# The order of TensorE's work in the Hyena stage of a hybrid encoder layer, written out by a count

## The chip, the cores and the metric

The kernel runs on one core of a Trainium2 chip. Its engines run side by side, each through its own instruction queue in order: TensorE (PE, matrix products; PEld is its weight load), VectorE (DVE), ScalarE (ACT), GpSimd (POOL), and SyncE (SP), which issues most of the transfers. The metric is the device time of one execution in microseconds (us).

## The reference

One layer on 1024 positions of 1024 channels, all in fp32 (cut):

```python
h = layer_norm(x) * (1 + scale) + shift          # scale, shift, gate from c @ w_ada
p = h @ w_in + b_in                              # 9216 columns: qkv, gates, hyena, merge gates
y_attn = dilated_window_attention(...) * silu(g_attn)        # three head groups
v, x1, x2 = split(centred_conv3(p_hy, conv_w, conv_b), 3)    # 512 channels each
filters = implicit_filters(...)                  # 3 sin layers, then @ w4, times a decay
z = v
for o, gate_o in enumerate((x1, x2)):
    z = gate_o * (circular_conv(z, filters[o]) + filt_bias[o] * z)   # FFT of size 2048
y_hy = z * silu(g_hy)
merged = sigmoid(r_attn) * (y_attn @ w_proj_attn) + sigmoid(r_hy) * (y_hy @ w_proj_hyena)
out = layer_norm(alpha * x + gate * (merged @ w_out + b_out)) * ln_g + ln_b
```

## The kernel before

The work runs in stages: normalising and transposing x (to about 61 us), the Hyena branch (61 to 640), attention (to 1244), merge and output (to the end). Every product that must be near fp32 is done in three products of a shorter format: each operand is split in a high and a low part (ScalarE casts the high part, another engine subtracts it), and high x high, high x low and low x high are summed.

**Projection tiles.** `proj` (L234) makes 128 columns of `h @ w_in`: the weights come by a 512 KB load (`load_w`, L226, two buffers), `split_w` (L217) casts them on ScalarE and subtracts on GpSimd (L223), then two halves of 24 matmuls of 512 columns (L242) go into one of three PSUM buffers and are evacuated by ScalarE. The Hyena stage holds 28 such tiles: 12 for v, x1, x2 (`conv_to_rows`, L583: bias, then a width-3 convolution of eight VectorE instructions, L608, then eight transposes, L612), 4 for the output gate (`silu_tile` in `out_gate`, L696) and 12 of the 16 merge gates (`gate_r`, L259, evacuated to `thr` and stored to DRAM).

**Filters.** `hidden` (L333) runs the three sin layers once, on VectorE, ScalarE and TensorE (L357, L359). `gen_filter` (L534) then makes each of four filters (two channel halves, two orders): eight products `px` (L560, L561) are multiplied by a decay table `dk` (L563) that is loaded in eight pieces of 256 KB with two buffers; sums and differences (`stage1`, L462) give eight complex pieces, "frequencies" j = -1 to 6; each is split (L499, L500, two negations L511, L512) and multiplied on TensorE with a table (`split_product`, L492; 6 matmuls of 512 columns, L521, or 12 of 256 for j = -1), scaled into `hs` and stored in DRAM.

**Convolutions.** `conv_order` runs `long_conv` (L615) four times. For each j in turn: the forward product of the piece (L521, or in full fp32 for j = -1, L531), the multiplication by the filter's spectrum on VectorE (L625 on), the split of the result and the inverse product, and sums of the inverse pieces. After j = 6 some 22 VectorE instructions build the eight row blocks, each multiplied into the next gate (L693).

**What sets the order.** The engines' instruction orders are made by a scheduler that takes whatever is ready by priority, which is the order of the code, and by assumed durations. The convolutions have a raised priority (`HIGH`, L52, L691), so that projections fill in on TensorE where the convolutions' inputs are not ready. Which tiles stand between which filters and convolutions is written at L719 to L749 (`GATES`, `FILLS` say how many merge gates). Tables: `tabf` (filters) and `tcon` (convolutions) share SBUF space, so `tcon` is loaded by GpSimd's queue after the last filter.

Of the kernel before, what the change touches and what calls it, by code (L numbers as in the profile page):

```python
# [42 lines left out]
FILLS = (3, 1, 4, 4)  # L43
GATES = (0, 3, 2)
# [7 lines left out]
HIGH = 20000  # L52
# [113 lines left out]

@with_exitstack
def hybrid_encoder(ctx, tc, A):
# [64 lines left out]

    def proj(n0, evac):  # L234

# [9 lines left out]
    def silu_tile(n0, sg, th_tile):  # L245

        hb = hbias[:, n0 // P : n0 // P + 1]

        def evac(half, ps, bias):
            sl = slice(512 * half, 512 * half + 512)  # L250
            th = th_tile()
            ACT.activation(th, ps, AF.Tanh, bias=hb, scale=0.5)
            ACT.activation(sg[:, sl], ps, AF.Identity, bias=hb, scale=0.5)
            V.scalar_tensor_tensor(sg[:, sl], th, 1.0, sg[:, sl], ALU.add, ALU.mult)

        proj(n0, evac)
        return sg

    def gate_r(j, th_tile):  # L259
# [8 lines left out]
        proj(n0, evac)  # L268


    with ExitStack() as st:
# [173 lines left out]
        def tt(a, b, op, out=None):  # L445
            o = pair() if out is None else out
            V.tensor_tensor(o, a, b, op)  # L447
            return o
# [7 lines left out]
        def stt(a, s, b, out=None):  # L456

            o = pair() if out is None else out
            V.scalar_tensor_tensor(o, a, s, b, ALU.mult, ALU.add)  # L459
            return o  # L460
# [31 lines left out]
        def split_product(j, y, tab, inverse, pool):  # L492


            z = ps_z.tile([P, 2, W], F32, name="z", tag="z")
# [4 lines left out]
            V.tensor_tensor(yl[:, c, :], y, yh[:, c, :].bitcast(F32), ALU.subtract)  # L500
            if j < 0:
                for i in range(2):
# [5 lines left out]
                    for k, (m, v) in enumerate(ops):  # L508
                        PE.matmul(z[:, i, :], m, v, start=k == 0, stop=k == 5)
                return z  # L510
            ACT.mul(yh[:, n, :], y[:, at, :], -1.0)  # L511
            ACT.mul(yl[:, n, :], yl[:, 2 * at, :].bitcast(F32), -1.0)  # L512
# [7 lines left out]
            for k, (m, v) in enumerate(ops):  # L520
                PE.matmul(z, m, v, start=k == 0, stop=k == 5)  # L521
            return z

        def conv_product(j, y, inverse):
            if j >= 0:
                return split_product(j, y, tcon, inverse, hy2)
            z = ps_z.tile([P, 2, W], F32, name="z", tag="z")
            for i in range(2):
                for q in range(2):
                    t = 4 * int(inverse) + 2 * i + q  # L530
                    PE.matmul(z[:, i, :], tcon0[:, t, :], y[:, q, :], start=q == 0, stop=q == 1)  # L531
            return z

        def gen_filter(hc, o):  # L534
# [5 lines left out]
            for e in range(2):  # L540
# [6 lines left out]
                V.tensor_tensor(wl, raw, wh.bitcast(F32), ALU.subtract)  # L547
                w4.append((wh, wl))
            fb = fl.tile([1, W], F32, name="fb", tag="fb")
            SY.dma_start(fb, A["filt_bias"][0][o : o + 1, cs])  # L550
            for a in range(0, 8, 2):
                for e in range(2):
# [4 lines left out]
                    wh, wl = w4[e]  # L557
                    for m in range(2):
                        hs = hid[e][:, a // 2, P * m : P * m + P]
                        PE.matmul(px[:, m, :], hs, wh, start=True, stop=False)  # L560
                        PE.matmul(px[:, m, :], hs, wl, start=False, stop=True)  # L561
                    b = a + 8 * e
                    V.tensor_tensor(g[:, b : b + 2], px, dk, ALU.mult)  # L563
                    if b == 0:
# [5 lines left out]
            for j, y in stage1(u, g[:, 8:12], g, g[:, 12:16], u, g[:, 8:12]):  # L570
                z = split_product(j, y, tabf, False, fl3)
# [11 lines left out]
        def conv_to_rows(ft, dst, co):  # L583


            u = hx.tile([P, S], F32, name="u", tag="u")
            y = hx.tile([P, S], F32, name="y", tag="yc")
            uv = _a_view(u)

            def evac(half, ps, bias):  # L590
                ACT.activation(uv[:, :, 8 * half : 8 * half + 8, :].rearrange("p t r i -> p r t i"),
                               ps.rearrange("p (r t i) -> p r t i", r=8, t=8), AF.Identity, bias=bias)

            proj(C_HY + P * ft, evac)
# [14 lines left out]
            for q in range(2):  # L609
                px = ps_x.tile([P, 512], F32, name="px", tag="px")  # L610
                for a in range(4):
                    PE.transpose(px[:, a * P : (a + 1) * P], y[:, (4 * q + a) * P : (4 * q + a + 1) * P], ident)  # L612
                ACT.copy(dst[:, 4 * q : 4 * q + 4, co : co + P], px.rearrange("p (a c) -> p a c", a=4))

        def long_conv(x, hc, o):  # L615
# [4 lines left out]
            for j, y in stage1(x[:, 0:4], x[:, 4:8], x, quad("s"), quad("d"), quad("q")):  # L620
                ht = hy2.tile([P, 2, W], F32, name="ht", tag="ht", bufs=1)
                SY.dma_start(ht, h_dram[hc, o, :, j + 1])
                z = conv_product(j, y, False)
# [4 lines left out]
                else:  # L628
# [3 lines left out]
                    V.tensor_tensor(p2[:, 1, :], z[:, 1, :], h0, ALU.mult)  # L632
                sub(p1[:, 0, :], p1[:, 1, :], p1[:, 0, :])
                add(p2[:, 0, :], p2[:, 1, :], p1[:, 1, :])
                v = conv_product(j, p1, True)
# [4 lines left out]

                if j == 0:
# [3 lines left out]
                    s = quad("t")  # L645
                    add(t, v, s[:, 0:2])
                    sub(t, v, s[:, 2:4])
                elif j == 2:
                    d = quad("s")
# [4 lines left out]
                elif j == 4:  # L654
                    ea, fa = add(vs[3], v, tmp()), sub(vs[3], v, tmp())
                elif j == 6:
                    eb, fb = add(vs[5], v, tmp()), sub(vs[5], v, tmp())
# [24 lines left out]
        def conv_x(hc, k, tag="xx"):  # L682
            pool, n = (hx, 2) if tag == "xx" else (hy, 1)
            x = pool.tile([P, 8, W], F32, name="xx", tag=tag, bufs=n)
            for c in range(2):
                conv_to_rows(4 * k + 2 * hc + c, x, P * c)
            return x

        def conv_order(x, z, hc, o):

            with tc.high_priority(offset=HIGH):  # L691
# [489 lines left out]
```

## Time and profile before

| | us |
|---|---|
| median of three runs (lowest, highest) | 1461.28 (1456.95, 1463.21) |
| the profiled execution | 1466.4 |
| its span, first to last instruction | 1464.6 |
| TensorE busy | 1351.3 (92%) |
| TensorE's weight loads | 1098.4 (75%) |
| VectorE busy | 957.6 (65%) |
| ScalarE busy | 624.4 (43%) |
| GpSimd busy | 282.2 (19%) |

The sums below are made in the time of the profiled execution, which is 5.1 us above the median. Matmul rows of TensorE overlap, and their ends are modelled; how many are issued per us tells more than how long they are busy. Line numbers are those of the kernel before.

### The profile page before, as it was taken

What the parts mean: (1) busy time and instruction counts of PE and PEld (TensorE: products, weight loads), DVE (VectorE), ACT (ScalarE), POOL (GpSimd) and SP (SyncE); (2) the same over time, 40 slices, a digit from 0 to 9 for tenths busy, and PEclk for the clock granted to TensorE, in tenths of its full rate; (3) what the DMA queues carried; (4) which work ended last, traced back from release to release, by engine and by line L of the source; (5) the groups of instructions that cost most, each with busy time, mean ns of one, the idle gap of its engine ahead of it and who ended that gap; (6) DMA issues with size and microseconds to landing.
All of it is one profiled execution on the core that took longest, in us unless ns stands there. A gap on an engine that the chain in (4) does not pass through costs nothing.

```text
span 1464.6 us, 18389 instructions
## 1 busy us (share of the span) xinstructions
PE 1351.3 (92%) x6707; PEld 1098.4 (75%) x6707; DVE 957.6 (65%) x1709; ACT 624.4 (43%) x1220; POOL 282.2 (19%) x160
## 2 busy tenths in 40 slices
PE   4788979889899999999999999999999999689997
PEld 1467767767777777788988788878887888567886
DVE  4798768767999898745156714761466144288866
ACT  1544444534244443446355534663466343242110
POOL 1221121210113122141121112111211111231220
PEclk9799999999999999999999999999999999899999
DMA  9633544332112222121113421311131114588523
GB/s 255 182 97 105 175 133 149 110 130 79 54 58 69 87 65 79 58 84 30 44 59 116 103 61 58 92 30 43 59 91 31 44 58 123 184 249 220 158 88 72
DMA packets 157024, 145.86 MB, mean 100 GB/s; under 512 B 16611, under 2 KB 126591, under 8 KB 156678
## 3 DMA queue, kind: packets, MB, share of 16 engines
q1 hardware_dynamic: 156486, 140.44, 32.7%
q0 software_dynamic: 288, 4.19, 0.8%
q8 instruction: 53, 0.87, 0.3%
q14 instruction: 37, 0.30, 0.1%
q10 hardware_dynamic: 160, 0.06, 0.0%
HBM read 116.73 MB, written 27.92 MB: 99 GB/s over the span
## 4 chain that ended last, share of the span: by engine, by line
PE 64%; DVE 11%; DMA 5%; ACT 3%; issue 2%; POOL 1%; SPq 0%; DVEq 0%; ACTq 0%; POOLq 0%
PE pj L242 33%; PE pj L888 6%; PE z L521 6%; PE po L1138 6%; PE pj L1103 4%; PE po L929 2%; PE pp L922 2%; DVE iv L447 2%; DVE f L447 1%; DMA dk<-in_t_dec 1%; DMA wor<-in_w_out 1%; PE z L531 1%; PE ss L859 1%; DVE f L459 1%; DVE q L447 1%
## 5 line engine op out<-in xcount | busy, mean ns | idle before, releaser
L223 POOL TENSOR_TENSOR wl<-wr,wh 128x1024 fp32r<-128x1024 f32 x88 | 234.8, 2668 | 966.9 <-ACT wh L222 895.7
L242 PE MATMUL pj<-hTh,wh 128*128 128x512 f32 x1024 | 407.5, 398 | 4.0 <-ACT hTh L433 4.0
L242 PE MATMUL pj<-hTl,wh 128*128 128x512 f32 x1024 | 407.1, 398 | 1.5 <-POOL hTl L435 0.8
L242 PE MATMUL pj<-hTh,wl 128*128 128x512 f32 x1024 | 408.1, 399 | 0.0
L242 PEld LDWEIGHTS pj<-hTl,wh 128*128 128x128 f32 x1024 | 194.3, 190 | 40.5 <-DVE hTl L435 2.2
L242 PEld LDWEIGHTS pj<-hTh,wh 128*128 128x128 f32 x1024 | 194.4, 190 | 39.9 <-ACT hTh L433 4.1
L242 PEld LDWEIGHTS pj<-hTh,wl 128*128 128x128 f32 x1024 | 194.4, 190 | 37.3 <-issue 1.0
L222 ACT CAST wh<-wr 128x1024 fp32r<-128x1024 f32 x88 | 92.4, 1050 | 239.5 <-PE pj L242 82.3
L499 ACT CAST yh<-f 128x512 fp32r<-128x512 f32 x88 | 54.1, 615 | 105.2 <-DVE f L447 93.9
L899 DVE TENSOR_TENSOR tmp<-pj,bv 128x512 f32<-128x512 f32 x16 | 11.1, 692 | 115.0 <-PE pj L888 115.0
L500 DVE TENSOR_TENSOR yl<-f,yh 128x512 fp32r<-128x512 f32 x88 | 65.6, 756 | 22.2 <-ACT yh L499 19.9
L521 PE MATMUL z<-yh,tcon 128*128 128x512 f32 x224 | 65.7, 411 | 8.6 <-ACT yh L499 8.6
L918 ACT ACTIVATE sx<-sx,stat 128x256 f32<-128x256 f32 (+1 forms) x128 | 71.6, 563 | 3.1 <-DVE stat L916 3.0
L916 DVE CUSTOM_DVE_ANT_0 sx<-ss,tab 128x384 f32<-128x384 f32 (+1 forms) x112 | 53.7, 492 | 29.2 <-PE ss L844 18.0
L888 PE MATMUL pj<-wh,hTh 128*128 128x256 f32 x256 | 72.7, 284 | 0.0
L888 PE MATMUL pj<-wl,hTh 128*128 128x256 f32 x256 | 72.6, 284 | 0.0
L888 PE MATMUL pj<-wh,hTl 128*128 128x256 f32 x256 | 72.6, 284 | 0.0
L925 DVE TENSOR_TENSOR pt<-pp,pt 128x256 fp32r<-128x256 f32 (+1 forms) x128 | 61.8, 486 | 14.9 <-ACT pt L924 13.6
L1103 PE MATMUL pj<-yh,wl 128*128 128x512 f32 x128 | 52.0, 406 | 17.8 <-ACT yh L1084 11.3
L924 ACT CAST pt<-pp 128x256 fp32r<-128x256 f32 (+1 forms) x128 | 52.2, 425 | 33.4 <-PE po L929 28.9
L922 PE MATMUL pp<-ident,sx 128*128 128x128 f32 x320 | 58.3, 280 | 4.2 <-DVE pt L925 2.7
L521 PEld LDWEIGHTS z<-yh,tcon 128*128 128x128 f32 x224 | 40.6, 191 | 22.3 <-ACT yh L499 15.0
(236 smaller groups left out, 2546.2 us busy)
## 6 DMA issues: line engine op xcount, KB each, us to landing
wr<-in_w_in SPq DMA_DIRECT2D x64, 512.0 KB
xt<-in_x SPq DMA_DIRECT2D x32, 256.0 KB
wa<-in_w_ada SPq DMA_DIRECT2D x16, 512.0 KB
dk<-in_t_dec SPq DMA_DIRECT2D x32, 256.0 KB
r_d<-thr SPq DMA_DIRECT2D x32, 256.0 KB
h_dram<-hs SPq DMA_DIRECT2D x32, 256.0 KB
ht<-h_dram SPq DMA_DIRECT2D x32, 256.0 KB
thr<-r_d SPq DMA_DIRECT2D x32, 256.0 KB
```

The costliest lines, as they stand in the source:

```text
L222: ACT.copy(wh[:, :k, :], src)
L223: PO.tensor_tensor(wl[:, :k, :], src, wh[:, :k, :].bitcast(F32), ALU.subtract)
L242: PE.matmul(ps, w[:, kt, :], h[:, kt, sl], start=i == 0, stop=i == len(ops) - 1)
L447: V.tensor_tensor(o, a, b, op)
L500: V.tensor_tensor(yl[:, c, :], y, yh[:, c, :].bitcast(F32), ALU.subtract)
L521: PE.matmul(z, m, v, start=k == 0, stop=k == 5)
L888: PE.matmul(ps[:, t % 2], h[:, 4 * q + k, P * t : P * t + P], w[:, 2 * k : 2 * k + 2, :], start=first and t % 2 == 0 and i == 0, stop=last ...
L918: ACT.activation(sx[:, : n * P], sx[:, : n * P], AF.Exp, bias=stat[:, t, e, 0:1], scale=-1.0, accum_out=stat[:, t, e, 1:2])
L922: PE.transpose(pp[:, a * P : (a + 1) * P], sx[:, a * P : (a + 1) * P], ident)
L925: V.tensor_tensor(pt[:, :n, 1, :], blk(pp), pt[:, :n, 0, :].bitcast(F32), ALU.subtract)
L1103: PE.matmul(ps, w[:, 4 * b + kt, :], y[:, kt, :], start=i == 0, stop=i == len(ops) - 1)
L1138: PE.matmul(po, m[:, P * q : P * q + P], w[:, kt, ds_], start=n == 0, stop=n == 23)
```

## The change

Three things change, all in the Hyena stage. (1) The order of TensorE's instructions there is that of the code (`manual_schedule` for TensorE alone; the other engines stay with the scheduler, and so does where instructions outside the region fall among those inside). The code emits them by a count: `clk` adds an assumed duration for each VectorE instruction and each matmul that it emits; before each filter or convolution product, `pace` pulls projection work, three matmuls at a time, out of a queue of tiles until TensorE's count reaches 1.03 times VectorE's plus 1 us or the queue is empty. The hidden layers stand ahead of the region and the count starts at zero behind them. Transposes of a tile are deferred into the middle of the next one, and there the next tile's weights are split. The raised priority goes. (2) In a convolution the forward product of frequency j is emitted ahead of the inverse product of j-1. (3) The low half of the weights is subtracted on VectorE instead of GpSimd, for the tiles of this stage. The number and shape of matmuls stay.

```diff
-FILLS = (3, 1, 4, 4)
-GATES = (0, 3, 2)
+GATES = (0, 4, 2, 2, 0, 4)
+RATIO = 1.03
+LAG = 1.0
-HIGH = 20000
-    def split_w(src):
+    def split_w(src, eng=None):
+        eng = eng or PO
         ACT.copy(wh[:, :k, :], src)
-        PO.tensor_tensor(wl[:, :k, :], src, wh[:, :k, :].bitcast(F32), ALU.subtract)
+        eng.tensor_tensor(wl[:, :k, :], src, wh[:, :k, :].bitcast(F32), ALU.subtract)
+    clk = {"pe": 0.0, "dve": 0.0}
+    def dve(ap):
+        clk["dve"] += 0.14 + 0.001065 * cols_of(ap)
+    def pe(n, passes=1):
+        clk["pe"] += 0.0133 + passes * n / 2400
+    queue, deferred, now = [], [], []
+    def prefetch(n0):
+        if n0 not in ready:
+            w = load_w(w_in[:, n0 : n0 + P])
+            ready[n0] = split_w(w, V)
+            dve(w)
+    def pull():
+        while now or queue:
+            if not now:
+                now.append(queue.pop(0)[1]())
+            if next(now[0], None):
+                return True
+            now.clear()
+        while deferred:
+            for _ in deferred.pop(0)():
+                pass
+        return False
+    def pace(lag=LAG):
+        while clk["pe"] < RATIO * clk["dve"] + lag and pull():
+            pass
+    def proj_steps(n0, evac):
+        prefetch(n0)
+        wh, wl = ready.pop(n0)
+        for half in range(2):
...
+            for i, (w, h, kt) in enumerate(ops):
+                PE.matmul(ps, w[:, kt, :], h[:, kt, sl], start=i == 0, stop=i == len(ops) - 1)
+                pe(512)
+                if i % 3 == 2:
+                    yield True
+            if half == 0:
+                if queue:
+                    prefetch(queue[0][0])
+                while deferred:
+                    yield from deferred.pop(0)()
+            evac(half, ps, cols[:, BIN + n0 // P : BIN + n0 // P + 1])
...
+        def split_product(j, parts, tab, inverse):
+            pace()
             z = ps_z.tile([P, 2, W], F32, name="z", tag="z")
+            yh, yl = parts
...
+                    pace()
                     for m in range(2):
                         hs = hid[e][:, a // 2, P * m : P * m + P]
                         PE.matmul(px[:, m, :], hs, wh, start=True, stop=False)
                         PE.matmul(px[:, m, :], hs, wl, start=False, stop=True)
+                        pe(2 * W)
...
+            r, p = {}, None
+            for j, y in stage1(x[:, 0:4], x[:, 4:8], x, quad("s"), quad("d"), quad("q")):
+                z = conv_product(j, conv_split(j, y, False), False)
+                if j >= 0:
+                    inverse(j - 1, p)
+                if j > 0:
+                    butterflies(j - 2)
+                p = spectrum(j, z)
+            inverse(6, p)
+            butterflies(5)
+            butterflies(6)
...
+        with tc.manual_schedule(engines={PE.engine}):
+            clk.update(pe=0.0, dve=0.0)
+            x0 = push_x(0, 0)
+            push_gates(GATES[0])
+            x1 = push_x(0, 1)
+            push_gates(GATES[1])
+            for hc, o in ((0, 0), (0, 1), (1, 0), (1, 1)):
+                gen_filter(hc, o)
+            need(x1)
+            fpool.close()
...
+            x2 = push_x(0, 2, "xx2")
+            push_gates(GATES[2])
+            z = conv_order(x1, need(x0), 0, 0)
+            x0 = push_x(1, 0)
+            push_gates(GATES[3])
+            z = conv_order(x2, z, 0, 1)
+            x1 = push_x(1, 1)
+            need(x0)
+            og = push_out(z, 0)
+            push_gates(GATES[4])
+            x2 = push_x(1, 2, "xx2")
+            z = conv_order(x1, need(x0), 1, 0)
+            need(og)
+            push_gates(GATES[5])
+            z = conv_order(x2, z, 1, 1)
+            push_out(z, 1)
+            push_gates(N_EARLY)
+            while pull():
+                pass
```

`push_x`, `push_gates` and `push_out` put tiles in the queue; `need(x)` pulls until x's two tiles are out. Every VectorE instruction of the stage has its `dve(...)` beside it, and every product its `pe(...)`.

## Rows read from the trace of the kernel before

**Rows 1.** The page's chain that ended last: shares of the span by engine.
```profile
PE 64%; DVE 11%; DMA 5%; ACT 3%; issue 2%; POOL 1%; SPq 0%; DVEq 0%; ACTq 0%; POOLq 0%
```

**Rows 2.** Stretches: length, busy us of PE, PEld, DVE, ACT, POOL; clock; DMA share, GB/s.
```profile
61.00:103.00 42.00, 36.67 (x135) 25.46 (x136) 41.53 (x70) 22.26 (x33) 10.42 (x6) 0.93 0.41 127
103.00:117.00 14.00, 11.37 (x54) 9.33 (x53) 10.80 (x18) 9.15 (x13) 2.56 (x1) 0.92 0.05 15
117.00:289.40 172.40, 154.07 (x707) 123.68 (x707) 136.94 (x202) 77.66 (x154) 32.50 (x19) 0.95 0.43 137
289.40:302.30 12.90, 7.85 (x39) 6.27 (x37) 6.20 (x8) 5.13 (x7) 2.91 (x2) 0.88 0.84 283
302.30:625.00 322.70, 302.25 (x1296) 237.88 (x1297) 270.68 (x467) 134.43 (x261) 55.16 (x17) 0.97 0.22 68
659.00:1244.00 585.00, 579.10 (x3353) 493.01 (x3353) 286.49 (x648) 299.44 (x652) 99.11 (x53) 1.00 0.24 65
```

**Rows 3.** The chain in order of time, a dense run: start, us, what, count.
```profile
685.60 29.73 PE pj L242 x131
```

**Rows 4.** TensorE, 61 to 117 us: xcount | busy us, mean ns | idle before, releasers.
```profile
L242 PE MATMUL pj<-hTl,wh 128*128 128x512 f32 x51 | 22.0, 438 | 1.5 <-POOL hTl L435 0.8 <-DVE hTl L435 0.5
```

**Rows 5.** TensorE's groups from 117 to 289.4 us, the filters.
```profile
L242 PE MATMUL pj<-hTl,wh 128*128 128x512 f32 x116 | 45.8, 395 | 0.0
...
L521 PE MATMUL z<-yh,tabf 128*128 128x512 f32 x112 | 37.7, 438 | 6.9 <-ACT yh L499 6.9
```

**Rows 6.** TensorE's groups from 302.3 to 625 us, the convolutions.
```profile
L242 PE MATMUL pj<-hTl,wh 128*128 128x512 f32 x274 | 109.0, 398 | 0.0
...
L521 PE MATMUL z<-yh,tcon 128*128 128x512 f32 x224 | 65.7, 411 | 8.6 <-ACT yh L499 8.6
L521 PE MATMUL z<-yl,tcon 128*128 128x512 f32 x112 | 41.3, 418 | 3.7 <-DVE yl L500 3.7
L531 PE MATMUL z<-f,tcon 128*128 128x256 f32 x64 | 20.9, 473 | 13.2 <-DVE f L447 8.0 <-DMA tcon<-in_t_con 5.1
```

**Rows 7.** VectorE in order of time, hidden layers: start, us, instruction.
```profile
79.57 0.80 DVE L362 TENSOR_SCALAR f<-px,fcol 128x512 f32<-128x512 f32 x1
...
81.68 2.58 DVE L364 TENSOR_SCALAR f<-f 128x512 f32<-128x512 f32 x1
...
95.14 3.18 DVE L608 SCALAR_TENSOR_TENSOR y<-u,cols,y 128x768 f32<-128x768 f32 x1
...
108.78 1.39 DVE L375 TENSOR_TENSOR hid<-f,hid 64x512 fp32r<-64x512 f32 x2
```

**Rows 8.** Tile dk: what its reader's engine waited for, us and times.
```profile
  DMA dk<-in_t_dec: 17.8, 13
```

**Rows 9.** VectorE in order of time, px stretch of the second filter.
```profile
164.13 1.29 DVE L563 TENSOR_TENSOR g<-px,dk 128x512 f32<-128x512 f32 x2 [3.83 <-PE px L561]
...
176.94 0.69 DVE L563 TENSOR_TENSOR g<-px,dk 128x512 f32<-128x512 f32 x1 [0.74 <-DMA dk<-in_t_dec]
```

**Rows 10.** The chain in order of time, between the last filter and the convolutions.
```profile
291.45 10.73 DMA tcon<-in_t_con
302.31 3.75 PE z L531 x8
```

**Rows 11.** VectorE's groups from 302.3 to 625 us, shapes apart.
```profile
L500 DVE TENSOR_TENSOR yl<-f,yh 128x512 fp32r<-128x512 f32 x56 | 43.7, 788 | 12.7 <-ACT yh L499 10.7
L447 DVE TENSOR_TENSOR f<-f 128x256 f32<-128x256 f32 x70 | 33.8, 485 | 0.1
```

**Rows 12.** VectorE and GpSimd in order of time, 458 to 468 us.
```profile
458.01 9.62 POOL L223 TENSOR_TENSOR wl<-wr,wh 128x1024 fp32r<-128x1024 f32 x1 [13.10 <-ACT wh L222]
...
460.05 1.28 DVE L459 SCALAR_TENSOR_TENSOR iv<-q,iv 128x512 f32<-128x512 f32 x2
...
462.45 2.35 DVE L447 TENSOR_TENSOR q<-xx 128x1024 f32<-128x1024 f32 x2
...
465.33 2.33 DVE L608 SCALAR_TENSOR_TENSOR y<-u,cols,y 128x7 f32<-128x7 f32 x1
```

More of the change, by code (lines that the diff above doesn't have):

```diff
@@ L232, in hybrid_encoder, with cols_of @@
     ready = {}
+    clk = {"pe": 0.0, "dve": 0.0}
+    def cols_of(ap):
+        n = 1
+        for k in ap.shape[1:]:
+            n *= k
+        return n
+    def dve(ap):
[26 more added lines that the diff above has]
+        for half in range(2):
+            ps = ps_w.tile([P, 512], F32, name="pj", tag="mm")
+            sl = slice(512 * half, 512 * half + 512)
+            ops = [(w, h, kt) for kt in range(KT) for w, h in ((wh, hTh), (wh, hTl), (wl, hTh))]
+            for i, (w, h, kt) in enumerate(ops):
[9 more added lines that the diff above has]
+            evac(half, ps, cols[:, BIN + n0 // P : BIN + n0 // P + 1])
     def proj(n0, evac):
@@ L243, in proj, with gate_evac @@
             evac(half, ps, cols[:, BIN + n0 // P : BIN + n0 // P + 1])
[L245 to L259, printed above, removed]
+    def gate_evac(j, th_tile):
         n0 = C_RA + P * j
@@ L680, in long_conv, with push_x, need, push_out @@
             yield slice(7, 4, -2), stt(d[:, 3:0:-2], -R2, e75, e75)
-        def conv_x(hc, k, tag="xx"):
+        def push_x(hc, k, tag="xx"):
+            x = {"left": 2}
             pool, n = (hx, 2) if tag == "xx" else (hy, 1)
-            x = pool.tile([P, 8, W], F32, name="xx", tag=tag, bufs=n)
             for c in range(2):
-                conv_to_rows(4 * k + 2 * hc + c, x, P * c)
-            return x
+                ft = 4 * k + 2 * hc + c
+                queue.append((C_HY + P * ft, lambda ft=ft, c=c: rows_steps(ft, x, pool, tag, n, c)))
+            return x
+        def need(x):
+            while x["left"] and pull():
+                pass
+            return x["x"]
         def conv_order(x, z, hc, o):
-            with tc.high_priority(offset=HIGH):
-                for a, y in long_conv(z, hc, o):
-                    V.tensor_tensor(x[:, a], y, x[:, a], ALU.mult)
-            return x
-        def out_gate(z, hc):
-            for c in range(2):
-                ft = 2 * hc + c
-                sg = hx.tile([P, S], F32, name="sg", tag="yc")
-                silu_tile(C_GH + P * ft, sg, lambda: hx.tile([P, 512], F32, name="thr", tag="thr", bufs=2))
+            for a, y in long_conv(z, hc, o):
+                xt = need(x)
+                V.tensor_tensor(xt[:, a], y, xt[:, a], ALU.mult)
+                dve(y)
+            return need(x)
+        def push_out(z, hc):
+            left = {"left": 2, "x": None}
+            def steps(c):
+                ft = 2 * hc + c
+                n0 = C_GH + P * ft
+                hb = hbias[:, n0 // P : n0 // P + 1]
+                sgs = []
+                def evac(half, ps, bias):
+                    if not half:
+                        sgs.append(hx.tile([P, S], F32, name="sg", tag="yc"))
+                    sg = sgs[0][:, 512 * half : 512 * half + 512]
+                    th = hx.tile([P, 512], F32, name="thr", tag="thr", bufs=2)
+                    ACT.activation(th, ps, AF.Tanh, bias=hb, scale=0.5)
+                    ACT.activation(sg, ps, AF.Identity, bias=hb, scale=0.5)
+                    V.scalar_tensor_tensor(sg, th, 1.0, sg, ALU.add, ALU.mult)
+                    dve(th)
+                yield from proj_steps(n0, evac)
                 yh = hx.tile([P, S], F32, name="yh", tag="u")
@@ L744, in hybrid_encoder, with note @@
-        z = conv_order(x1, x0, 1, 0)
-        fill(FILLS[2])
-        z = conv_order(x2, z, 1, 1)
-        fill(FILLS[3])
-        out_gate(z, 1)
-        fill(16)
+                    n0, evac = gate_evac(j, lambda: hx.tile([P, 512], F32, name="thr", tag="thr", bufs=2))
+                    queue.append((n0, lambda n0=n0, evac=evac: proj_steps(n0, evac)))
+        def note(what):
+            if DEBUG:
+                print(what, {k: round(v, 1) for k, v in clk.items()}, "queued", len(queue), "now", len(now))
```

135 lines of the change are left out of this document (80 added, 55 removed).

## The prediction

> **What bounds the kernel now.** I read the chain of waits first: two thirds of it is TensorE, a ninth VectorE [rows 1]. Then the busy times by stage [rows 2]: from 659 to 1244 us (attention) TensorE is busy 579 of 585 us, so what the Hyena stage saves or loses ahead of it moves the end by as much. The change touches only what lies between 61 us (the first projection product) and about 659.
>
> How full TensorE really is there I take from counts, because a matmul's row lasts 398 ns [rows 6] while a dense run issues 131 of them in 29.73 us [rows 3]: 0.227 us each. A 256-column one and a transpose I put at half, 0.12; a hidden-layer product in full fp32 at double, 0.45; an L531 product at half of the 0.47 that eight of them show at the lower clock [rows 10], 0.24. From 117 to 289.4 us (four filters) there are 3x116 projection products, 112+56 on the filter table [rows 5], by the code some 124 px products and 48 more of 256 columns, and 19 transposes: 79.0+38.1+20.6+2.3 = 140 us of work in 172.4, so 32.4 lost. From 302.3 to 625 (four convolutions): 3x274x0.227 + 336x0.227 + 64x0.24 [rows 6] + 74 transposes x 0.12 = 287.2 of 322.7, so 35.5 lost. In the same way 9.5 are lost from 61 to 103, 3.7 from 103 to 117 (153 projection products together [rows 4]) and 5.3 from 289.4 to 302.3; from 625 on, where attention's products take over, none. Sum: 86.4 us. By 625 all 28x48 = 1344 projection products of the stage are out (153+348+822 and 31 in the short stretch, ten of them attention's already).
>
> The busy row alone would give the convolutions 20 us to win (302.25 busy of 322.7 [rows 2]). The Trainium skill (Trainium Kernel Development and Optimization, "Performance Expectations") holds matmul busy time for a bad measure of TensorE and weight-load busy time for a good one; weight loads are busy 73.7% there against 84.3% in attention [rows 2], which by that rule leaves 41 us idle. The count's 35.5 lies nearer to it; with 20 the sum below would come out 15 us worse.
>
> **The change, part by part.** TensorE's own work stays: 28 tiles of 48 products, the same filter and convolution products and transposes. So I ask place by place what becomes of the 86.4 us.
>
> *The fill rate.* A product now waits in the code until TensorE's count has reached 1.03 times VectorE's plus 1. The count charges VectorE 0.14+0.001065 per column: 0.685 us for 512 columns, 0.41 for 256, 1.23 for 1024. Two 512-column instructions in a row take 1.28, two of 1024 2.35 [rows 12]; VectorE is some 5 to 10% faster than its count, and TensorE is handed 0.706 us of work per 0.64. By count the filters hold 4x31.2 us of VectorE work, four row tiles at 3.3 and six weight splits at 1.23: 145.5, target 150.9. The queue (8 tiles, 87 us), filter products (58) and transposes (4) make 149, so the queue runs out just at their end. Each convolution counts 62.3; with rows, gates and splits the targets at the four ends are 227, 303, 394, 463 against 217, 285, 379, 445 us of available work. So TensorE has work nearly always, and it is the slower of the two.
>
> *Start, 61 to 117 us.* Now TensorE does 153 projection products ahead of the first px product, while VectorE runs the hidden layers, 79.57 to 110.2 [rows 4, 7]. In the new order nine stand ahead of it (target 1.03x0.83+1 = 1.85 us, three pulls of 0.68), and it needs the hidden layers. Everything of the region is queued behind it on TensorE; attention's products, which may pass, have no free weight buffer and no place to be evacuated to. The hidden layers end earlier: the short-convolution instructions leave that stretch (8.1 us between 79.57 and 110.2, with a stall of some 2 in the 3.18 at 95.14), and so does the stall in the 2.58 at 81.68: 110.2-8.1-2 = 100. From 61 to 100 TensorE does 12 hidden products (5.4 us) and nine others (2.0) and loses 31.6. Bounds: 27 (a chain 4 us shorter) and 41 (it still ends near 110).
>
> *Filters.* Eight px steps each need a 256 KB decay load with two buffers. In the second filter they take 13.5 us (164.13 to 177.6), and VectorE waited 17.8 us in all for these loads [rows 8, 9]. The count knows no loads: in such a stretch TensorE gets 3.8 us of px products and 2 of fill, and no projection may pass a waiting px product, with all of the stage behind it. Loss 7.7, four times 30.8. The rest of a filter is dense: 37.3 us of work less 5.8 is 31.5, VectorE's part of it about 26. One us per filter I add for the clock, granted at 0.95 in this stretch and at 1.00 where TensorE is full [rows 2]: 34.8. Bounds: 15 (row instructions and splits, with their fill, fall into the load waits) and 55 (each wait also costs several us at the lower of the clock's two levels, and products wait for casts as now, 6.9 us [rows 5]).
>
> *Between filters and convolutions.* The constants' load takes 10.73 us and the first product waits for it [rows 10]; the fill by then is 4.5 us. Loss 6, bounds 3 and 11.
>
> *Convolutions.* Now TensorE idles 13.2 us ahead of L531 and 12.3 ahead of L521 [rows 6]; the rest is lost at products issued singly and at the clock. Between the forward product of a frequency and its inverse now stand another inverse and another forward product (1.4 us each) and about 4 us of fill; the link that must fit in has four multiplications and sums (1.9 us), a cast, a difference and two negations, some 4 to 5 us. Between two orders VectorE alone works some 15 us (25 instructions of 0.34 to 1.2), and the fill there is 12.5, then 20, then 15 us. I keep 3 us at the first of these joints and 7 for stray waits: 10. Bounds 3, and 36 (as now).
>
> *Weight splits on VectorE.* 26 splits of 1024 columns at 1.2 us [rows 12] are 31 us more on VectorE, queued in its order; a tile's low half can be late by what is ahead of it. Against it, GpSimd's splits held VectorE: a 7-element instruction took 2.33 us beside a split that took 9.62 itself [rows 12]. Means over undisturbed durations in the convolutions (0.788 against 0.68, times 56; 0.485 against 0.415, times 70 [rows 11]; smaller groups 16 more) sum to 27 us for 17 splits, 1.6 each. Net on VectorE: -10 us, nothing on the path while TensorE is the slower; without that cover -10 to +31. SP's weight loads need only a free buffer and keep their place; gate stores move with their tiles; GpSimd's load commands and copies no longer stand behind splits.
>
> Sum of the losses: 31.6+34.8+6+10 = 82.4 against 86.4: 4 us less. The profiled execution took 1466.4 us (span 1464.6), so 1462.4. It lay 5.1 above the median of 1461.3; I forecast 1457.
>
> **Rivals.**
> 1. *The filters fill up.* Row and split instructions, which bring their own fill, come into the load waits, and the filters lose 15 instead of 35. For it: the fill is spread by VectorE's count, and four row tiles and six splits have to fall somewhere. Against: their share of the count is a seventh. Time 1457-20 = 1437.
> 2. *The fixed order stalls the convolutions* (slower). Place: a product whose split is late, with all fill behind it. Price: 36 us lost instead of 10, so 1483. It decides when the link from a forward product to its inverse exceeds the 7 us of TensorE work between them; VectorE's order, chosen ahead by assumed durations and now without the raised priority, need only put a 3 us row block or two splits into the link. For it: VectorE is busy 270.7 of 322.7 us already [rows 2]. Against: a tenth of slack.
> 3. *VectorE becomes the bound.* Its work there, 270.7-27+24 (20 splits) = 268, would have to pass the 319 us that TensorE then has (287 and three tiles more). It needs a fifth more; if waits between engines make that up, the time is about that of 2.
>
> **How the numbers follow.** Forecast 0.40, its own range 1448 to 1466; rival 1 0.30; rivals 2 and 3 0.30. A difference within 0.5% (7 us) can't be told from none. A third of the forecast's chance lies below 1454: faster 0.30+0.11 = 0.41, same 0.27, slower 0.32. All bounds together would be 48 and 143 us of loss, but they don't meet; the range reaches 25 us below the forecast and 29 above, 1432 to 1486.
>
> **What would show it.** Right: TensorE all but idle from some 64 to 100 us; the last filter product near 283 instead of 289, with 8 tiles done instead of 10.4; gaps of 6 to 9 us in the four px stretches, behind VectorE's L563, itself behind the decay load; convolutions with weight loads near 83% busy; no 7-element VectorE instruction over 0.3 us. Wrong: projection products during the hidden layers; no px gaps (then 1); L521 still idling 8 us or more for ScalarE's cast in the convolutions (then 2).

## The result, and the profile after

The changed kernel took 1502.26 us (median of 4 runs, 1499.67 to 1503.98), the kernel before 1462.24 beside it (4 runs): ratio 1.0279, 95% interval 1.0248 to 1.0309. It is 40 us slower; 1457 was predicted, and the range ended at 1486.

The prediction's count of "lost" time (length of a stretch less TensorE's work in it, at 0.227 us per full product) gives 126.3 us for the profiled execution after (1499.67 us, span 1497.9), against 86.4 before: 39.9 more. The two profiles, each from its first projection product (61.4 us before, 56.0 after) to its end, differ by 38.7 us, so the count holds the whole difference. From 659 to 1244 us nothing changed (TensorE busy 579.1 us before, 579.6 after). So the question is where TensorE stood.

Line numbers from here on are those of the kernel whose trace is shown. In the changed kernel L584, L599, L684 and L693 answer to L521, L531, L608 and L612 of the kernel before, L498 and L511 to its L447 and L459.

The stretches after, which answer to [rows 2] (length; busy us of PE, PEld, DVE, ACT, POOL; clock; DMA share, GB/s):

```profile
56.00:96.60 40.60, 15.49 (x21) 6.05 (x21) 37.59 (x67) 16.77 (x25) 5.61 (x4) 0.58 0.34 108
96.60:291.00 194.40, 164.71 (x755) 133.27 (x756) 141.76 (x222) 86.31 (x166) 19.24 (x12) 0.94 0.37 118
291.00:299.40 8.40, 6.76 (x30) 5.25 (x28) 3.93 (x6) 0.69 (x1) 0.54 (x1) 1.00 0.96 342
299.40:632.00 332.60, 298.94 (x1306) 238.19 (x1307) 256.48 (x473) 138.89 (x264) 0.00 (x0) 0.97 0.23 71
659.00:1244.00 585.00, 579.55 (x3337) 493.46 (x3335) 280.75 (x632) 301.57 (x643) 107.60 (x64) 1.00 0.23 62
```

| stretch | lost before | forecast | lost after |
|---|---|---|---|
| start, to the first px product | 13.2 (to 117 us) | 31.6 | 33.3 |
| filters | 32.4 | 34.8 | 45.3 |
| between filters and convolutions | 5.3 | 6 | 1.8 |
| convolutions, to their last transposes | 35.5 | 10 | 45.9 (43.9 + 2.0) |

Against the kernel before, half of the 39.9 us lies at the start (20.1), where the prediction had foreseen it; the filters add 12.9 and the convolutions 10.4. Against the forecast most of the difference lies in the convolutions: 35.9 of 43.9 us.

By the busy row the convolutions lose 34 us (332.60 less 298.94); their weight loads are busy 238.19 of 332.60, 71.6%, less than before, where 83% had been forecast.

What TensorE waited for from 55 to 660 us after (us in total, times, longest):

```profile
PE px L693 <- DVE y L684: 22.8, 7, 12.4
PE px L410 <- ACT f L419: 19.2, 2, 15.4
PE z L584 <- ACT yh L550: 19.0, 15, 2.6
PE px L631 <- DVE g L635: 15.5, 13, 5.1
PE px L631 <- DVE hid L426: 5.4, 1, 5.4
```

Line 693 is the transpose of a row tile; it leads the list, and the prediction gave it no term. (The second and the fifth row are the start.) TensorE's groups in the convolutions, 299.4 to 632 us (count | busy, mean ns | idle before, and what ended it), stand beside [rows 6]:

```profile
L584 PE MATMUL z<-yh,tcon 128*128 128x512 f32 x221 | 62.1, 402 | 13.9 <-ACT yh L550 13.8
L584 PE MATMUL z<-yl,tcon 128*128 128x512 f32 x110 | 36.9, 406 | 0.2
L599 PE MATMUL z<-f,tcon 128*128 128x256 f32 x64 | 15.2, 380 | 1.7 <-DVE f L498 1.7
L693 PE MATMUL px<-ident,y 128*128 128x128 f32 x64 | 9.3, 294 | 19.6 <-DVE y L684 19.6
```

In the kernel before, the transposes of the row tiles (302.3 to 625 us) had no idle time ahead of them:

```profile
L612 PE MATMUL px<-ident,y 128*128 128x128 f32 x56 | 9.1, 273 | 0.0
```

Of the idle time that the forecast counted as saved, two parts are saved: 13.2 to 1.7 us ahead of the full-fp32 products (z<-f, j = -1), 3.7 to 0.2 ahead of the low-half ones. But the high-half ones idle 13.9 instead of 8.6, and the transposes 19.6. In all TensorE idles 35.4 of the 43.9 us lost in this stretch; before it idled 25.5 of 35.5. The rest, 8.5 and 10.0 us, is lost without idle time, with the clock at 0.97 both times.

Of the high-half waits, told apart by the order of the code, 8.9 us stand ahead of forward products. The other 4.9 stand ahead of the last inverse product (j = 6) of the second and the fourth convolution:

```profile
441.37 1.35 PE L584 MATMUL z<-yh,tcon 128*128 128x512 f32 x4 [2.33 <-ACT yh L550]
631.72 1.20 PE L584 MATMUL z<-yh,tcon 128*128 128x512 f32 x4 [2.52 <-ACT yh L550]
```

All other inverse products waited for nothing.

The longest of these waits, TensorE in order of time (start, us, instruction, idle before it):

```profile
549.08 0.39 PE L289 MATMUL pj<-hTh,wl 128*128 128x512 f32 x1
561.87 1.51 PE L693 MATMUL px<-ident,y 128*128 128x128 f32 x6 [12.41 <-DVE y L684]
```

VectorE in the same time:

```profile
546.97 1.01 DVE L684 SCALAR_TENSOR_TENSOR y<-u,cols,y 128x768 f32<-128x768 f32 x1
547.90 0.68 DVE L498 TENSOR_TENSOR iv<-iv 128x512 f32<-128x512 f32 x1
548.50 0.41 DVE L684 SCALAR_TENSOR_TENSOR y<-u,cols,y 128x192 f32<-128x192 f32 x1
...
557.47 0.27 DVE L684 SCALAR_TENSOR_TENSOR y<-u,cols,y 128x56 f32<-128x56 f32 x1
557.65 1.22 DVE L498 TENSOR_TENSOR q<-xx 128x1024 f32<-128x1024 f32 x1
558.79 0.23 DVE L684 SCALAR_TENSOR_TENSOR y<-u,cols,y 128x7 f32<-128x7 f32 x1
...
561.13 0.74 DVE L684 SCALAR_TENSOR_TENSOR y<-u,cols,y 128x192 f32<-128x192 f32 x3
```

VectorE never rests here. The row tile's eight short-convolution instructions (line 684, 3.2 us in one piece) are spread over 15 us, each behind a few instructions of the convolution's tail (lines 498, 511, 806). TensorE's list has the tile's transposes next, and with all other work of the stage behind them it stands 12.41 us. This tile is the extreme: the eight instructions of the other eleven take 3.3 to 5.1 us from first to last, and the six other waits for transposes are 0.6 to 3.3 us long. The chain that ended last, followed back, ends at this place; its oldest long pieces are:

```profile
561.21 0.67 DVE y L684 x3
561.88 1.93 PE px L693 x8
563.81 16.81 PE pj L289 x71
```

The start, TensorE in order of time. Nine projection products, four of the features, then the hidden layers one by one with nothing between them:

```profile
61.10 3.62 PE L408 MATMUL px<-feat,w 66*128 66x512 f32 x4
80.13 3.78 PE L410 MATMUL px<-f,w 128*128 128x512 f32 x4 [15.41 <-ACT f L419]
87.68 3.50 PE L410 MATMUL px<-f,w 128*128 128x512 f32 x4 [3.77 <-ACT f L419]
96.63 0.58 PE L631 MATMUL px<-w4h,hid 128*128 128x256 f32 x1 [5.44 <-DVE hid L426]
```

### The profile page after: what moved, and what is told of

Read it like the earlier page. It is cut to its first block, busy times and chain, and to the rows that moved or that the text cites. A ratio compares the mean times of both kernels' runs of the same rounds, so it can differ in the third digit from the quotient of the medians.

```text
span 1497.9 us, 18388 instructions
## 1 busy us (share of the span) xinstructions
PE 1351.6 (90%) x6707; PEld 1100.4 (73%) x6707; DVE 943.6 (63%) x1735; ACT 625.4 (42%) x1220; POOL 211.1 (14%) x134
## 4 chain that ended last, share of the span: by engine, by line
PE 51%; DVE 4%; DMA 3%; ACT 2%; issue 2%; POOL 0%; SPq 0%; DVEq 0%; ACTq 0%; POOLq 0%
PE pj L307 24%; PE pj L1041 6%; PE po L1291 6%; PE pj L1256 4%; PE pj L289 3%; PE po L1082 2%; PE pp L1075 2%; DMA wor<-in_w_out 1%; PE z L584 1%; ACT sx L1071 1%; PE ss L1012 1%; PE ss L1013 1%; DMA wr<-in_w_ada 1%; PE ss L997 1%; DVE iv L498 1%
## 5 line engine op out<-in xcount | busy, mean ns | idle before, releaser
L228 POOL TENSOR_TENSOR wl<-wr,wh 128x1024 fp32r<-128x1024 f32 x62 | 154.1, 2486 | 933.6 <-ACT wh L227 846.4
L551 DVE TENSOR_TENSOR yl<-f,yh 128x512 fp32r<-128x512 f32 x88 | 60.2, 690 | 28.2 <-ACT yh L550 22.9
L584 PE MATMUL z<-yh,tcon 128*128 128x512 f32 x224 | 62.8, 402 | 13.9 <-ACT yh L550 13.8
L1071 ACT ACTIVATE sx<-sx,stat 128x256 f32<-128x256 f32 (+1 forms) x128 | 71.6, 563 | 3.1 <-DVE stat L1069 3.0
```

What stands on the lines that cost most here:

```text
L228: eng.tensor_tensor(wl[:, :k, :], src, wh[:, :k, :].bitcast(F32), ALU.subtract)
L1071: ACT.activation(sx[:, : n * P], sx[:, : n * P], AF.Exp, bias=stat[:, t, e, 0:1], scale=-1.0, accum_out=stat[:, t, e, 1:2])
```

## The experiments

**Theories.** A: part 1 makes TensorE stand at the head of its own list, at places where VectorE's order, which the scheduler still chooses, has the operand late; the row tiles' transposes are the dearest. B: the loss is mostly the start, where nothing covers the hidden layers. C: VectorE's extra work (part 3) is the cause. D: the convolutions' pipelining (part 2) doesn't pay.

What was measured, in the order of the sections below; "lost" is by the count above, from the first projection product to the last transpose of the stage, in one profile each:

| kernel | median us | ratio to before, 95% | lost | first projection at |
|---|---|---|---|---|
| changed | 1502.3 | 1.0279 (1.0248-1.0309) | 126 | 56.0 |
| 1 rows led at the start | 1509.9 | 1.0312 (1.0269-1.0354) | 127 | 63.8 |
| 2 short convolution ahead | 1479.8 | 1.0130 (1.0068-1.0192) | 106 | 53.7 |
| 3 transposes later | 1497.1 | 1.0217 (1.0173-1.0261) | 118 | 62.2 |
| 4 splits on GpSimd | 1537.7 | 1.0510 (1.0467-1.0554) | 160 | 58.9 |
| 5 gates led at the start | 1499.6 | 1.0244 (1.0189-1.0300) | 112 | 58.3 |
| 6 = 5 + 2 | 1492.6 | 1.0195 (1.0140-1.0249) | 102 | 63.5 |
| 7 before + part 3 | 1450.8 | 0.9922 (0.9892-0.9952) | 68 | 60.9 |
| 8 before + part 2 | 1460.0 | 0.9981 (0.9949-1.0012) | 83 | 58.7 |
| 9 before + parts 2, 3 | 1445.3 | 0.9863 (0.9829-0.9896) | 59 | 62.6 |
| 10 changed, order lifted | 1432.6 | 0.9798 (0.9760-0.9836) | 60 | 54.9 |
| 11 = 9 + short convolution ahead | 1419.5 | 0.9712 (0.9667-0.9757) | 37 | 58.0 |
| 12 = 10 + short convolution ahead | 1418.2 | 0.9694 (0.9675-0.9712) | 40 | 61.9 |

**1. Rows led at the start.** Projection work of the hyena rows is pulled ahead of the first filter, three of the late gate tiles moved forward to make up for it.

```diff
-GATES = (0, 4, 2, 2, 0, 4)
+GATES = (0, 7, 2, 2, 0, 1)
...
+            for _ in range(44):
+                pull()
+            clk.update(pe=0.0, dve=0.0)
```

> The changed kernel, but 44 pulls (132 projection products, 30 us) are emitted ahead of the first filter, the count set back to zero behind them, and three merge gates moved from the last convolution's queue to the filters' (GATES 0,7,2,2,0,1), so that the fill per stage stays. Theory A (TensorE stands idle during the hidden layers because the first px product is ahead of all projections in a fixed order; in the trace of the changed kernel TensorE loses 33 us from 56 to 97 us, before it lost 13 up to the first filter): the loss falls to about 13, time 1502 - 20 = 1482. Rival B (the stage's length is set by VectorE and waits between engines, TensorE's idle start costs nothing): 1502 within 6.

1509.9, no gain: against theory B. The hole is filled, but the first px product comes 55.1 us after the first projection instead of 40.6, since the led rows' instructions take VectorE from the hidden layers; the start loses 18.5 us instead of 33.3, the convolutions 57.5 instead of 45.9. The casts are waited for longer later (TensorE's waits from 63 us):

```profile
PE z L584 <- ACT yh L550: 23.3, 15, 3.5
PE px L693 <- DVE y L684: 22.1, 6, 12.9
...
PE px L410 <- ACT f L419: 5.1, 3, 3.9
```

**2. The short convolution ahead.** The row tiles' ScalarE instruction and eight VectorE ones are given a raised priority, so that VectorE does them as one piece as soon as the projection is there; TensorE's list stays.

```diff
+            with tc.high_priority(offset=20000):
-            ACT.activation(y, u, AF.Identity, scale=w[1], bias=cols[:, CB + ft : CB + ft + 1])
+                ACT.activation(y, u, AF.Identity, scale=w[1], bias=cols[:, CB + ft : CB + ft + 1])
...
-                V.scalar_tensor_tensor(a, b, w[k], a, ALU.mult, ALU.add)
+                    V.scalar_tensor_tensor(a, b, w[k], a, ALU.mult, ALU.add)
```

> The changed kernel, but the width-3 convolution of the rows (ScalarE's y and the eight VectorE instructions) gets a raised priority. Theory A (the transposes, now fixed in the middle of the next tile, wait for VectorE, which does these instructions late; 24.8 us lost in eight such waits in the trace, 2.8 before): the waits of px<-ident,y fall below 8 us, time 1502 - 15 to 20 = 1482 to 1487. Rival B (the lost time moves to the products, since VectorE's convolution work is then late): px<-ident,y falls, z<-yh,tcon rises by as much, time 1502 within 6.

1479.8: 22.5 us less than the changed kernel, a little more than theory A expected. VectorE, at the corresponding place, does the row tile's eight instructions without a break:

```profile
536.84 0.68 DVE L511 SCALAR_TENSOR_TENSOR q<-iv 128x512 f32<-128x512 f32 x1
537.44 3.25 DVE L685 SCALAR_TENSOR_TENSOR y<-u,cols,y 128x768 f32<-128x768 f32 x8
540.62 0.68 DVE L498 TENSOR_TENSOR iv<-iv 128x512 f32<-128x512 f32 x1
```

TensorE's waits from 54 to 640 us of this run:

```profile
PE z L584 <- ACT yh L550: 16.7, 14, 2.5
...
PE px L694 <- DVE y L685: 6.9, 7, 1.8
```

The transposes' waits fall from 22.8 to 6.9; the casts' (19.0 to 16.7) hardly move. Of these 16 us, 11.6 are the one long wait, 12.4 us before and 0.8 now.

**3. Transposes later.** The other way to give VectorE time: the deferred transposes come out at the end of the next tile instead of in its middle.

```diff
-                while deferred:
-                    yield from deferred.pop(0)()
+            while half and deferred:
+                yield from deferred.pop(0)()
```

> The changed kernel, but a tile's transposes are emitted at the end of the next tile instead of its middle, 24 products (5.4 us or more) later. Theory A (the place in TensorE's order is too early): of 24.8 us lost ahead of px<-ident,y some 10 remain (the one wait of 12.4 us still 5 or more), time 1502 - 12 = 1490. Rival B (rows come later, and the next tile's rows wait for the one buffer y): loss moves on, 1502 within 6 or above.

1497.1, 5 us less. Transposes lose 11 instead of 26 by the count, as theory A expected, but other waits take back some 6, so that the time is 7 us above its 1490; one wait of 7.0 us ahead of the transposes is left. A later place in a fixed list moves the bet, it doesn't remove it.

**4. Splits back on GpSimd** (part 3 undone, order and counts kept).

```diff
-            ready[n0] = split_w(w, V)
+            ready[n0] = split_w(w, PO)
```

> The changed kernel with the low half of the weights back on GpSimd; TensorE's order and count unchanged. Theory A (VectorE is not the slower engine, so the split's place costs little; GpSimd held VectorE 1.6 us per split before, a split on VectorE takes 1.2): time 1502 to 1510. Rival B (the 31 us of splits on VectorE are what makes it late for transposes and products): 1502 - 15 to 25 = 1477 to 1487.

1537.7: 35 us slower than the changed kernel; both expectations missed, and theory C falls. The transposes wait still longer:

```profile
PE px L693 <- DVE y L684: 35.6, 8, 14.6
```

One cause shows in VectorE's group for the low halves of the convolution, its same 128x512 form, first of the changed kernel, then of this one (from 299 to 640 us, where this run's convolutions are not yet done: 48 of 56; over all 56 the mean is 878 ns):

```profile
L551 DVE TENSOR_TENSOR yl<-f,yh 128x512 fp32r<-128x512 f32 x56 | 38.3, 688 | 7.5 <-ACT yh L550 5.9
```
```profile
L551 DVE TENSOR_TENSOR yl<-f,yh 128x512 fp32r<-128x512 f32 x48 | 43.5, 910 | 14.2 <-ACT yh L550 13.3
```

A mean of 910 ns beside GpSimd's splits (2.59 us each) against 688 with the splits (1.22 us) in VectorE's own queue. The Trainium skill (SBUF — State Buffer, "Who interferes with whom") says that a VectorE instruction with two SBUF inputs contends with a GpSimd instruction that reads SBUF; these two groups agree. The whole stage shows the sum, first of the changed kernel, then of this one (columns as in [rows 2]):

```profile
55.98:659.02 603.04, 511.27 (x2229) 403.43 (x2230) 456.46 (x796) 248.92 (x466) 30.24 (x18) 0.94 0.29 92
58.89:695.54 636.65, 525.96 (x2229) 413.18 (x2230) 465.11 (x770) 249.86 (x466) 89.37 (x44) 0.92 0.27 87
```

VectorE has 26 splits fewer to do (31.7 us in the changed kernel) and is yet busy 8.7 us longer: its other 770 instructions take some 40 us more beside GpSimd's splits. How much of the 35 us comes by that way, and how much by the splits' own lateness, was not separated.

**5. Gates led at the start.** Three merge-gate tiles, which leave VectorE nothing but a split, go ahead of the first filter.

```diff
-N_EARLY = 12
+N_EARLY = 15
...
-        for n0 in (C_HY, C_HY + P):
+        for n0 in (C_RA, C_RA + P):
...
+            push_gates(3)
...
+            for _ in range(48):
+                pull()
+            clk.update(pe=0.0, dve=0.0)
```

> The changed kernel with three tiles of the merge gate led ahead of the first filter (their weights split ahead in place of those of the hyena rows, 48 pulls of them before the fixed order begins to count); a gate tile leaves nothing for VectorE but its weight split, so that the hidden layers are not held up as by led rows. Theory (the start is a hole that any work of TensorE fills): the loss of 33 us at the start falls to some 10, the three tiles of 10.9 us leave the stretch after the convolutions, 1502 - 22 = about 1480. Rival (what is led only moves the hidden layers back, as led rows did): 1500 +- 6.

1499.6, 3 us less instead of 22; the intervals of the two ratios overlap, so this is not told from no difference. The time is the rival's, and so is part of its mechanism: the start loses 10.0 us instead of 33.3, as the theory expected, but the first px product comes 50.2 us after the first projection instead of 40.6, and the filters lose 56.2 instead of 45.3. The stage itself is 13.7 us better (621.7 us less 32.7 of gate work, against 602.7), but the rest shrinks by 20.4 us only, not by the 32.7 that were taken out of it. The gates were filler ahead of the output projection, whose one wait doubles. TensorE's waits after the stage, first of the changed kernel, then of this one:

```profile
PE pj L1256 <- ACT yh L1237: 9.5, 1, 9.5
```
```profile
PE pj L1260 <- ACT yh L1241: 19.1, 1, 19.1
```

**6. Gates led and the short convolution ahead** (edits 5 and 2 together).

> The three led gate tiles together with the rows' short convolution put ahead on VectorE and ScalarE (that part alone measured 1480). Theory (start and late rows are separate losses, their gains add): 1480 - 22 = about 1458, a little under the kernel before. Rival (the rows put ahead take VectorE from the filters and the convolutions, and that eats the gain): 1475 to 1485.

1492.6: the gains don't add; it is slower than edit 2 alone. Counted from the first projection its profile ends after 1427.6 us, that of edit 2 after 1421.7; the rest of the difference of the two profiles is the later first projection (63.5 against 53.7). In the stage it loses 102 us against 106, but behind the stage the time shrinks by 23.1 us only, again not by 32.7. The start is filled (8.4 us lost), but the filters lose 53.2 us (40.6 in edit 2) and transposes 18.9 again (8.3). In this fixed order a hole that was filled opened again elsewhere. Theory B alone doesn't explain the 40 us: the start's share is 20, and leading work brought at most 14 of them back in the stage (edit 5).

**7. Part 3 alone** in the kernel before.

```diff
...
+        split_eng[0] = V
         x0 = conv_x(0, 0)
         gen_filter(0, 0)
...
         fill(16)
+        split_eng[0] = PO
```

> The kernel before, in the scheduler's order, with one part of the change alone: the weight splits of the hyena stage on VectorE. Theory (the splits on GpSimd keep VectorE out and come late, as the fixed order showed, where putting them back cost 35 us): faster, 1435 to 1450. Rival (the scheduler's order takes whatever is ready and so hides late splits; the splits then only add to VectorE's work): 1460 to 1475.

1450.8: 11 us faster by medians, the interval below 1, and just short of what the theory expected.

**8. Part 2 alone** in the kernel before.

```diff
...
+            for j, y in stage1(x[:, 0:4], x[:, 4:8], x, quad("s"), quad("d"), quad("q")):
+                z = conv_product(j, y, False)
+                if j >= 0:
+                    inverse(j - 1, p)
+                if j > 0:
+                    butterflies(j - 2)
+                p = spectrum(j, z)
...
```

> The kernel before, in the scheduler's order, with one part of the change alone: the convolution products pipelined by one frequency. Theory (the wait of the inverse product for its spectrum, 17 us of TensorE's loss before, is filled by the next forward product): 1440 to 1450. Rival (the scheduler already fills it with projections as far as there are any, and the order of the tiles' reuse adds waits): 1460 +- 5.

1460.0: no measurable difference, as the rival expected.

**9. Parts 2 and 3 without part 1** (edits 7 and 8 together).

> Parts 2 and 3 of the change without part 1: the scheduler orders TensorE as before, the convolution products are pipelined by one frequency and the stage's weight splits are on VectorE. Theory (part 1, the order by a count, is what costs; parts 2 and 3 each gain or do nothing in the scheduler's order, -2 and -11 us alone, and the changed kernel's time less this one's is the price of part 1): 1445 to 1452, part 1 costs about 50 us. Rival (pipelining and splits on VectorE get in each other's way, both load VectorE's queue in the convolutions, and the loss is no matter of the order): 1465 or more.

1445.3: parts 2 and 3 together are 1.4% faster than before, so adding part 1 to them costs 57 us (1502.3 less 1445.3). Theories C and D are out as causes of the loss; part 2 alone, though, did not pay either.

**10. The order lifted.** Program, counts and tiles of the changed kernel, but the scheduler may pass over an instruction whose operand is late.

```diff
-        with tc.manual_schedule(engines={PE.engine}):
+        with ExitStack():
             clk.update(pe=0.0, dve=0.0)
```

> The changed kernel with the same program text, counts and tiles, but the fixed order of TensorE lifted: the scheduler may pass over an instruction whose operand is late. Theory (the loss is TensorE standing at the head of its own list while later work is ready): TensorE's loss from 126 us to 70 to 90, time 1445 to 1470. Rival (the loss comes from how the emission spreads the tiles, which stays as it is): 1490 to 1505.

1432.6: 70 us less than the changed kernel by one line, more than expected, and 2% under the kernel before. Theory A. By the count some 66 us come back: 19.6 at the start, 21.1 in the filters, 27.7 in the convolutions (the joint between them loses 1.9 more). Its groups in the convolutions, 275 to 570.5 us:

```profile
L584 PE MATMUL z<-yh,tcon 128*128 128x512 f32 x224 | 64.5, 400 | 0.2 <-ACT yh L550 0.2
...
L599 PE MATMUL z<-f,tcon 128*128 128x256 f32 x64 | 18.3, 423 | 8.6 <-DVE f L498 5.2 <-DMA tcon<-in_t_con 3.5
L693 PE MATMUL px<-ident,y 128*128 128x128 f32 x56 | 8.2, 296 | 0.2 <-DVE y L684 0.2
```

Transposes 19.6 to 0.2, high halves 13.9 to 0.2: whenever one of these was late, something else was ready. It is not that VectorE delivers sooner: the eight instructions of a row tile take 3.3 to 18.2 us from first to last here, 98.6 for the twelve tiles together, against 55.4 in the changed kernel. In the kernel before they took 6.3 to 21.9 us, and TensorE idled 2.6 us ahead of transposes in the whole stage.

Whether the emission by count helps as an order of preference is not shown. By medians this run is 12.7 us under edit 9, but both lose some 60 us by the count and their stages are equally long (536.7 and 536.2 us); of the 13.3 us between the two profiles, 7.7 are the earlier first projection and 6.1 lie behind the stage.

**11. Edit 9 with the short convolution ahead.**

> Parts 2 and 3 in the scheduler's order, with the rows' short convolution put ahead as in the run that brought the fixed order 22 us. Theory (late rows cost only where TensorE can't pass over them): within 4 us of parts 2 and 3 alone, 1445 to 1452. Rival (late rows delay whatever the order is): 10 to 20 us faster than parts 2 and 3 alone.

1419.5: 26 us less than edit 9, and here the rival was right: late rows cost in the scheduler's order too. By the count 22 us come back, and most of them ahead of the convolutions: 11.0 at the start (first px product 46.5 us after the first projection instead of 52.9), 7.1 in the filters, 3.3 between filters and convolutions. Within the convolutions transposes (3.9 us) and the full-fp32 products (z<-f, 10.3) lose nothing any more, but the high-half products lose 15.8 instead of 4.8, so that of 17.7 us 16.7 remain.

**12. The order lifted and the short convolution ahead** (edits 10 and 2).

> The changed kernel with the fixed order lifted and the rows' short convolution put ahead: whether the two cures add. Theory (two separate losses: rows late on VectorE are late for any order, and the fixed order adds its own stalls): 1432.6 less 15 to 25 us, 1408 to 1418. Rival (with the order lifted nothing waits for rows any more, transposes lose 1.5 us there, and rows ahead only push the filters and convolutions back): 1430 to 1437.

1418.2: the two cures add (14 us under edit 10, a little less than the theory's lower end), and it beats both kernels: 0.9694 of the time before (0.9675 to 0.9712). It is no different from edit 11 (1419.5), which does without part 1. The convolutions of this run:

```profile
285.30:560.20 274.90, 274.20 (x1218) 219.96 (x1219) 247.38 (x455) 131.36 (x255) 0.00 (x0) 1.00 0.27 86
```

TensorE is busy all but 0.7 us and loses 4.4 by the count, with weight loads busy 80.0%; VectorE is at 90%.

## Why the prediction was wrong

Its sum was 82.4 us of loss; 126.3 came. The terms in turn:

- **What bounds it:** right. Each us lost in the stage is one us of the whole: 39.9 by the count, 38.7 between the profiles from the first projection product on.
- **Start:** right: 31.6 forecast, 33.3 measured, nine projection products ahead of the first px product, and that one 40.6 us after the first projection product (39 forecast).
- **Filters:** 34.8 forecast, 45.3 measured, inside its bounds. The px stretches are as described: VectorE waits 16.5 us for decay loads (17.8 in [rows 8]) and they lose 7.4, 4.5, 8.1 and 5.1 us, 25.1 in all against 30.8 forecast (6 to 9 each). The "dense" rest loses 20 instead of 4: casts, transposes behind rows, the clock at 0.94. So the last filter product ended 234 us after the first projection product, where 222 was forecast.
- **Between filters and convolutions:** 6 forecast, 1.8 measured.
- **Convolutions: this is the step that failed.** "I keep 3 us at the first of these joints and 7 for stray waits: 10": it was 45.9, outside the bounds of 3 and 36. The link from a product to its inverse, on which the step argued, did get its cover (no inverse product but the last of a convolution waited). What the step left out is every other instruction in TensorE's list that needs another engine: the rows' transposes, which wait for VectorE (19.6 us of idle time), and the casts ahead of forward products and of two last inverses (13.9). It also put at nothing what is lost without idle time, 10.0 us before and 8.5 after, which alone nearly fills its 10.
- **Fill rate:** the stock was right (8.0 tiles done at the last filter product, as the count had it) and did not help. In the long waits work stood behind the late instruction in TensorE's list; it could not be reached. The count adds up how much VectorE has to do, and VectorE does it in another order: the scheduler's, in which one row tile's eight instructions were spread over 15 us among the convolution's tail.
- **Splits on VectorE:** "nothing on the path" was mis-sized: 11 us gained alone (edit 7), 35 lost when taken back in the fixed order (edit 4). The 7-element instruction is 0.23 us at most, as the prediction's sign for it asked.
- **Rivals:** rival 2 had the side and the mechanism (a fixed order that stalls) but the wrong place, a late weight split, and 36 us as its price. Its sign came true (high-half products idle 13.9 us for the cast, 8 or more had been named), but not at the link that was to decide it. It had named the row block as something that gets into the link; at the longest wait it was the convolution's tail that got into the row block. Rival 3 did not come: VectorE is busy 256.5 of 332.6 us in the convolutions. (In the sum of the chances a third of 0.40 is 0.13, not 0.11.)

The Trainium skill (TensorE: Matmul & The Clock Gate, "Step-by-step: what each phase is for") states that matmuls stay in program order. The 12.41 us ahead of the transposes agree, and edit 10 shows the price: what stands behind a late instruction was ready, and used when it might pass.

Open is how much of edit 4's 35 us is contention. A third and fourth buffer for the decay loads was not tried, there being no room for them; so the px stretches' 25 us in the fixed order were not split by experiment. With the order lifted (edit 10) the filters lose 24.2 us in all instead of 45.3.

## What to carry to other kernels

An order fixed by hand for one engine is a bet on when the other engines deliver; check it at each instruction that needs another engine, not by totals of work. Where a scheduler can pass over what is late, let it: here the same program went from 1502 to 1433 us by that alone. And look for small producers (3 us of VectorE work per row tile) that are queued late or in pieces among a long chain: putting them ahead gave 14 to 26 us in every order tried without led work.

## What was not expected of the hardware

The first projection product started anywhere from 53.7 to 63.8 us in the 13 profiles of the table (61.4 in the one before), although no edit changes how much work lies ahead of it (edits 5 and 6 load and split two other weight tiles there, of the same size). Why is open; profiles are therefore best compared from there. TensorE's granted clock was 0.58 in the stretch where it stood for the hidden layers (1.2 GHz is half, 2.4 GHz full), and 0.94 in the same stretch of edit 12, where projections filled it:

```profile
61.90:105.70 43.80, 41.88 (x156) 30.19 (x156) 42.98 (x77) 22.71 (x33) 5.67 (x4) 0.94 0.39 120
```
